# The entry of the MLP of a hybrid decoder block: a written order for ScalarE and VectorE, five operations on GpSimd, and another first product

## The chip, the cores and the metric

The kernel runs on one core of one Trainium2 chip. The metric is the device time of one execution in microseconds. A core has TensorE (matmuls, which read SBUF and write PSUM), VectorE and ScalarE (elementwise work on SBUF and PSUM), GpSimd (elementwise work on SBUF; it also issues some DMAs) and SyncE (which issues the other DMAs). Each engine works through its own queue in order and waits on semaphores of the others.

## The reference

One decoder layer on a sequence of 1024 tokens with 1024 channels, float32. Only the end of it matters here:

```python
mix = jnp.concatenate([att, conv, pool], axis=-1)
x = x + mix @ w_out[l]
h2 = rms_norm(x, norm2_g[l])
up = h2 @ w_up[l]                       # 1024 x 5632
up = causal_depthwise_conv(up, ffn_dw_w[l])   # width 3
gate, val = jnp.split(up, 2, axis=-1)
x = x + (jax.nn.silu(gate) * val) @ w_down[l]
```

## The kernel before

Products of float32 are made of three matmuls (`mm3`, lines 53 to 55): each operand is split into a rounded high half and the rest, the low half (`split`: line 48, a cast on ScalarE; line 49, a subtraction, on VectorE unless another engine is given), and high x high, high x low and low x high are added up in PSUM.

The up-projection of the MLP is made block by block: `up(f)` for 22 blocks `f` of 128 gate and 128 value channels. Each block's four quarter products (two halves of the tokens, two halves of the channels) are made from seven products instead of eight, by sums and differences of the quarters (a Strassen scheme). So the activations are needed in four raw quarters and in differences of them: `hq["11"]`, `hq["2"]`, `hq["3"]` and `hq["21"]` hold t1, t2, t3 and t4, and `T[q]` holds the split (high, low) pairs that TensorE reads: `t11`, `t21` (raw, first half of the tokens), `t22` (raw, second half), `t1`, `t2`, `t3`, `t4`. On the weights' side `wur` is a block as loaded, `wuh`/`wul` its split raw quarters, `ws` its sums and differences, `wsh`/`wsl` the split of these. One product is `prod`: four channel chunks of three matmuls, twelve matmuls of 128x512.

Ahead of the blocks stands the entry, a loop over eight token tiles `t` of 128 tokens (`c` in the profile is the output projection's last part, `x` and `x2s` its residual sum). `h2T(t)` normalises a tile and transposes it:

- line 702, the tile is stored to DRAM by GpSimd's queue; line 704, its square sum on ScalarE; lines 85 and 86, the inverse root on GpSimd (`ss`); line 706, the normalised tile `xh` on VectorE;
- line 712, eight transposes on TensorE into two PSUM banks (`d` in the profile, `pq[0]` and `pq[1]` in the code), four each;
- for tiles 0 to 3 the splits of t11 and t21 and a copy; for tiles 4 to 7 a copy to t3 (line 722, ScalarE), t1 (a subtraction, line 677), the split of t22, then t2, t3 and t4 (subtractions, line 677). In the profile all four arrays are called `h`; in the lists of order below they are `h_5422` (t1), `h_5428` (t2), `h_5429` (t3) and `h_5423` (t4).

The two transpose banks are used in turn, so a tile's transposes wait until the tile before has been read from the same bank.

At the last tile, before its `h2T`, block 0's two products that need only the first tokens are issued (t11 and t21), and the columns of the first three late tiles (0:384) of t2, t1 and t3 are split. The last 128 columns are split in `up(0)`, together with `ws` and t4. Block 0 then makes the products t2, t1, t3, t22, t4. The PSUM pool `psO` of the odd blocks takes the banks that the transposes leave.

The order on each engine is set by a scheduler which places the instructions by its own timeline and by the order in which they are written; an engine in a `manual_schedule` keeps the written order. The written order holds on SyncE alone, and there only in the down-projection. Pools have a fixed number of buffers per tag (`s8` six, `ep` four, `hx` eight, `mx` two and four), and a buffer is taken again when its last reader is done.

Of the kernel before, what the change touches and what calls it, by code (L numbers as in the profile page):

```python
# [16 lines left out]
P = 128  # L17
# [22 lines left out]
def tile_hybrid_block(ctx: ExitStack, tc: tile.TileContext, x: bass.AP, xT: bass.AP, prm: bass.AP,  # L40
# [635 lines left out]
    def sub(out, a, b):  # L676
        nc.vector.tensor_tensor(out=out, in0=a, in1=b, op=ALU.subtract)  # L677
# [17 lines left out]
    def psum(f):  # L695
        pool = psE if f % 2 == 0 else psO
        return [pool.tile([P, 512], F32, name=n, tag=n) for n in ("b1", "b2", "b3")]

    def h2T(t):
        xh = cp.tile([P, D], F32, name="xh")  # L700
        xs = x2[t // 2][:, (t % 2) * D:(t % 2) * D + D]
        nc.gpsimd.dma_start(out=x2d[t], in_=xs)
        ss = cp.tile([P, 1], F32, name="ss2")
        nc.scalar.activation(out=xh, in_=xs, func=AF.Square, accum_out=ss)
        rsqrt(ss, ss, D, 1)
        nc.vector.scalar_tensor_tensor(out=xh, in0=xs, scalar=ss, in1=g2b, op0=ALU.mult, op1=ALU.mult)
        ts = slice((t % 4) * P, (t % 4) * P + P)
        pq = []
        for q in range(2):
            ps = psD.tile([P, 512], F32, name="d", tag="d")  # L710
            for j in range(4):
                nc.tensor.transpose(out=ps[:, j * P:(j + 1) * P], in_=xh[:, (q * 4 + j) * P:(q * 4 + j + 1) * P],
                                    identity=ident)
            pq.append(ps.rearrange("p (k n) -> p k n", k=4))
        if t < 4:
            for q, quad in enumerate(("11", "21")):
                hi, lo = T[quad]
                split(hi[:, :, ts], lo[:, :, ts], pq[q])
                nc.scalar.copy(out=hq[quad][:, :, ts], in_=pq[q])
        else:  # L720
            t1, t2, t3, t4 = [hq[q][:, :, ts] for q in ("11", "2", "3", "21")]
            nc.scalar.copy(out=t3, in_=pq[0])
            sub(t1, pq[0], t1)
            hi, lo = T["22"]
            split(hi[:, :, ts], lo[:, :, ts], pq[1])
            sub(t2, pq[1], t1)
            sub(t3, pq[1], t3)
            sub(t4, t4, t2)

    SKEW = 2  # L730
    load_up(0)
# [3 lines left out]
    for t in range(NT):  # L735
        mix_att(t, 1)
        if t + SKEW < NT:
            mix_att(t + SKEW, 0)
        if t == NT - 1:
            bank0 = psum(0)  # L740
            prod(bank0[0], hl[0][0], 0, "11", True, True)
            prod(bank0[1], hl[0][0], 1, "21", True, True)
            T["2"] = (slot(s8, "s8", "t2h", F32R), slot(s8, "s8", "t2l", F32R))
            T["1"] = (slot(s8, "s8", "t1h", F32R), slot(s8, "s8", "t1l", F32R))
            T["3"] = (slot(s8, "s8", "t3h", F32R), slot(mxa, "mx", "t3l", F32R))
            for q, src in (("2", "2"), ("1", "11"), ("3", "3")):
                split(T[q][0][:, :, 0:384], T[q][1][:, :, 0:384], hq[src][:, :, 0:384])
# [5 lines left out]


    ep = mlp.enter_context(tc.tile_pool(name="ep", bufs=4, **left))
    psO = ps_ctx.enter_context(tc.tile_pool(name="psO", bufs=1, space=PSUM))

    def ex(name, dtype=F32):
        return slot(ep, "ep", name, dtype)

    def split_sums(f):
        hi, lo = ex("wsh", F32R), ex("wsl", F32R)
        split(hi, lo, ws[f])
        hl[f].append((hi, lo))

    def taps3(ac, us, e, f):
        w0 = PC_FW + (e * NF + f) * 3
# [3 lines left out]
                                           op0=ALU.mult, op1=ALU.add)  # L771

    def up(f):
        b1, b2, b3 = bank0 if f == 0 else psum(f)
        raw_hl = hl[f][0]
        u = ex("u").rearrange("p (e h) n -> p e (h n)", e=2)
        ug, uv = u[:, 0], u[:, 1]
# [4 lines left out]
        if f > 0:  # L782
            prod(b2, raw_hl, 1, "21", True, True)
        nc.vector.tensor_tensor(out=ug[:, h0], in0=ug[:, h0], in1=b2, op=ALU.add)
        if f == 0:
            split_sums(0)
            r = slice(384, 512)
            split(T["2"][0][:, :, r], T["2"][1][:, :, r], hq["2"][:, :, r])
            split(T["1"][0][:, :, r], T["1"][1][:, :, r], hq["11"][:, :, r])
            split(T["3"][0][:, :, r], T["3"][1][:, :, r], hq["3"][:, :, r])  # L790
# [247 lines left out]
```

## Time and profile before

| | |
|---|---|
| median of 3 runs | 1162.03 us (1159.37 to 1162.38) |
| profiled execution | 1161.21 us, its span 1159.4 us |
| busy in the span | TensorE 1104.9, VectorE 882.5, ScalarE 576.0, GpSimd 361.4 us |
| granted TensorE clock, mean | 0.982 |
| entry: tile 4's transposes to block 1's first product of sums | 480.9 to 526.1 us |
| TensorE busy from 526.1 to 926 | 398.7 of 399.9 us |

Times in the rows of a timeline are microseconds from the start of the span: start, length, engine, line, operation, output and inputs by the program's names, shapes, a count where several like instructions stand in one row, and in brackets how long the engine had been idle before, and for whom it waited. In rows of groups the columns are the line, engine, operation, names and shapes with a count, then busy time and the mean of one in ns, then the idle time before.

### The profile page before, as it was taken

Reading aid. Unit: us, or ns where it says so; the run is one execution under the profiler, and the core shown is the slowest. Engines: PE = TensorE matmul, PEld = TensorE weight load, DVE = VectorE, ACT = ScalarE, POOL = GpSimd, SP = SyncE. Lnnn points to the kernel's source line nnn. Section 1 sums busy time; section 2 is a strip of 40 time slices with the busy share of each in tenths; the row PEclk is TensorE's granted clock in tenths of the full one; section 3 lists DMA queues with packets and bytes.
Section 4 is the critical chain, followed back from the end, with each engine's and each line's share of the span. In section 5 each row is a group of like instructions: output and inputs, shape, how many; then the busy total and the mean of one; then the engine's idle time right before and its main releaser. Section 6 shows DMA issues by size and latency. Waiting matters only on the chain.

```text
span 1159.4 us, 15556 instructions
## 1 busy us (share of the span) xinstructions
PE 1104.9 (95%) x5684; PEld 921.4 (79%) x5684; DVE 882.5 (76%) x1259; ACT 576.0 (50%) x1045; POOL 361.4 (31%) x373
## 2 busy tenths in 40 slices
PE   7999889999999999879999999999999999899996
PEld 6789889978778878758888888888888788688875
DVE  5798974758998756778877888787878755998673
ACT  8322456688998644445443535353535343233331
POOL 1365597867666653101212121212121210000010
PEclk9999999999999999969999999999999999899999
DMA  9220110022111141211222121312221397672372
GB/s 359 72 81 25 40 28 20 15 74 74 55 48 46 47 154 73 109 37 55 89 75 96 68 96 68 105 59 85 79 98 67 117 328 267 240 263 91 128 235 74
DMA packets 51885, 119.99 MB, mean 103 GB/s; under 512 B 6368, under 2 KB 11872, under 8 KB 48992
## 3 DMA queue, kind: packets, MB, share of 16 engines
q1 hardware_dynamic: 46208, 99.06, 25.8%
q0 software_dynamic: 5600, 19.93, 4.3%
q8 instruction: 45, 0.74, 0.3%
q14 instruction: 32, 0.26, 0.1%
HBM read 94.84 MB, written 19.92 MB: 99 GB/s over the span
## 4 chain that ended last, share of the span: by engine, by line
PE 69%; DVE 10%; issue 7%; DMA 5%; ACT 4%; POOL 3%; SPq 1%; POOLq 0%; ACTq 0%; DVEq 0%
PE b L53 12%; PE b L55 12%; PE b L54 12%; PE mm L53 3%; PE mm L55 3%; PE mm L54 3%; DVE dl L49 3%; PE s L499 2%; DVE acc L257 2%; PE t L523 2%; DMA dr<-in_w_down_dram 2%; PE c L53 1%; PE c L55 1%; PE c L54 1%; DMA dr<-gd 1%
## 5 line engine op out<-in xcount | busy, mean ns | idle before, releaser
L814 POOL TENSOR_TENSOR ac<-ac 128x1024 f32<-128x1024 f32 x22 | 61.5, 2793 | 367.9 <-ACT u L795 207.3
L770 DVE SCALAR_TENSOR_TENSOR ac<-u,par,ac 128x1023 f32<-128x1023 f32 x88 | 112.7, 1280 | 9.6 <-ACT ac L768 8.7
L53 PE MATMUL mm<-w,hh 128*128 128x256 f32 (+1 forms) x384 | 110.3, 288 | 8.5 <-DVE qk L445 4.6
L54 PE MATMUL mm<-w,hh 128*128 128x256 f32 (+1 forms) x384 | 109.5, 285 | 0.6 <-POOL w L49 0.6
L55 PE MATMUL mm<-w,hl 128*128 128x256 f32 (+1 forms) x384 | 109.1, 284 | 0.0
L48 ACT CAST wsh<-ws 128x2048 fp32r<-128x2048 f32 x22 | 42.0, 1910 | 123.5 <-PE b L54 123.3
L257 DVE SCALAR_TENSOR_TENSOR acc<-u,par,acc 128x512 f32<-128x512 f32 x120 | 93.3, 835 | 0.0
L49 DVE TENSOR_TENSOR dl<-dr,dh 128x1024 fp32r<-128x1024 f32 (+1 forms) x39 | 65.6, 1684 | 28.0 <-ACT dh L48 24.9
L511 POOL TENSOR_TENSOR p<-p,l 128x896 f32<-128x896 f32 (+3 forms) x64 | 72.6, 1151 | 44.0 <-DVE l L510 37.5
L48 ACT CAST dh<-dr 128x1024 fp32r<-128x1024 f32 (+1 forms) x39 | 54.7, 1401 | 58.4 <-PE y L55 24.7
L53 PEld LDWEIGHTS mm<-w,hh 128*128 128x128 f32 x384 | 73.0, 190 | 10.1 <-DVE fgt L433 4.8
L49 POOL TENSOR_TENSOR w<-wr,w 128x256 fp32r<-128x256 f32 (+1 forms) x56 | 63.9, 1166 | 42.6 <-ACT w L48 42.3
L54 PEld LDWEIGHTS mm<-w,hh 128*128 128x128 f32 x384 | 73.1, 190 | 1.2 <-POOL w L49 0.8
L55 PEld LDWEIGHTS mm<-w,hl 128*128 128x128 f32 x384 | 73.2, 191 | 0.3
L864 POOL DMA_DIRECT2D out_dram<-acc x16 | 8.7, 542 | 206.9 <-DVE acc L860 206.3
L54 PE MATMUL x<-dl,dh 128*128 128x512 f32 x176 | 69.6, 395 | 3.4 <-DVE dl L49 3.4
L55 PE MATMUL x<-dh,dl 128*128 128x512 f32 x176 | 69.3, 394 | 0.0
L768 ACT ACTIVATE ac<-u,par 128x1024 f32<-128x1024 f32 x44 | 50.7, 1152 | 36.3 <-DVE u L805 35.8
L48 ACT CAST dh<-res 128x1024 fp32r<-128x1024 f32 x22 | 23.1, 1051 | 84.2 <-PE y L55 55.7
L49 DVE TENSOR_TENSOR wsl<-ws,wsh 128x2048 fp32r<-128x2048 f32 x22 | 50.4, 2290 | 12.4 <-ACT wsh L48 12.4
L677 DVE TENSOR_TENSOR ws<-wur 128x512 f32<-128x512 f32 x22 | 59.1, 2688 | 0.0
L53 PE MATMUL x<-dh 128*128 128x512 f32 x176 | 54.0, 402 | 5.2 <-DVE acc L860 4.5
(308 smaller groups left out, 3395.1 us busy)
## 6 DMA issues: line engine op xcount, KB each, us to landing
wur<-in_w_up_dram SPq DMA_DIRECT2D x22, 1024.0 KB, 4.9
dr<-in_w_down_dram SPq DMA_DIRECT2D x66, 256.0 KB, 5.1
dr<-gd SPq DMA_DIRECT2D x55, 256.0 KB, 4.3
gd<-ac POOLq DMA_DIRECT2D x22, 512.0 KB, 3.0
res<-gd SPq DMA_DIRECT2D x22, 256.0 KB, 5.6
wr<-in_w_in_dram SPq DMA_DIRECT2D x40, 128.0 KB, 2.1
v<-in_x_dram SPq DMA_DIRECT2D x8, 512.0 KB, 8.4
wor<-in_w_out_dram SPq DMA_DIRECT2D x16, 256.0 KB, 3.0
```

Of the source, the lines that this page charges most:

```text
L48: nc.scalar.copy(out=dst_hi, in_=src)
L49: (lo or nc.vector).tensor_tensor(out=dst_lo, in0=src, in1=dst_hi.bitcast(F32), op=ALU.subtract)
L53: nc.tensor.matmul(ps, a_hi, b_hi, start=first, stop=False, skip_group_check=more)
L54: nc.tensor.matmul(ps, a_hi, b_lo, start=False, stop=False, skip_group_check=more)
L55: nc.tensor.matmul(ps, a_lo, b_hi, start=False, stop=last, skip_group_check=more)
L257: nc.vector.scalar_tensor_tensor(out=a, in0=u[:, c, o + j:o + j + 512], scalar=pc(PC_DW + c * CW + j), in1=a, op0=ALU.mult, op1=ALU.add)
L499: nc.tensor.matmul(ps[:, 0:c1 - c0], qT[:, i * P:(i + 1) * P], part[:, c0:c1], start=b == 0, stop=b == 1 and c1 < n)
L511: nc.gpsimd.tensor_tensor(out=pt[:, 0:n], in0=pt[:, 0:n], in1=l[:, 1:2].broadcast_to([P, n]), op=ALU.mult)
L677: nc.vector.tensor_tensor(out=out, in0=a, in1=b, op=ALU.subtract)
L768: nc.scalar.activation(out=ac, in_=us, func=AF.Copy, scale=pc(w0 + 2))
L770: nc.vector.scalar_tensor_tensor(out=ac[:, j:S], in0=us[:, 0:S - j], scalar=pc(w0 + 2 - j), in1=ac[:, j:S], op0=ALU.mult, op1=ALU.add)
L814: nc.gpsimd.tensor_tensor(out=a[:, 1], in0=a[:, 1], in1=a[:, 0], op=ALU.mult)
```

## The change

From the last token tile on, ScalarE and VectorE get the written order (`manual_schedule`), which ends inside `up(0)`. `last_tile` writes it out: the split of block 0's `ws` first, its low half on GpSimd; then the old columns of t2; then the last tile's own steps with t22 and t2 ahead of t3 and t1. For tiles 4 to 7 the difference of t4 goes to GpSimd (four operations of 128x512). t1 is split behind t2, t3 whole (2048 columns) in `up(0)`, behind the load and the raw split of block 1, which `up(0)` now has ahead of its products. Block 0's product t22 comes first, into a PSUM bank of its own (`b22`, in `psO`, whose waits are now by tile), and is added to `u` by one more VectorE operation. `wsh`/`wsl` of all blocks move from pool `ep` to `s8`, t3's split pair from `s8` and `mx` to `ep`, t1's low half to `mx`.

```diff
@@ h2T
+        if t == NT - 1:
+            return pq
...
-            sub(t4, t4, t2)
+            nc.gpsimd.tensor_tensor(out=t4, in0=t4, in1=t2, op=ALU.subtract)
+
+    def split_sums(f, lo=None):
+        pair = slot(s8, "s8", "wsh", F32R), slot(s8, "s8", "wsl", F32R)
+        split(*pair, ws[f], lo)
+        hl[f].append(pair)
+
+    banks, region = [], ExitStack()
+
+    def last_tile(t):
+
+        old, new = slice(0, 384), slice(384, 512)
+        banks.extend(psum(0))
+        T["2"] = (slot(s8, "s8", "t2h", F32R), slot(s8, "s8", "t2l", F32R))
+        T["1"] = (slot(s8, "s8", "t1h", F32R), slot(mxa, "mx", "t1l", F32R))
+        (h2, l2), (h1, l1), (h22, l22) = T["2"], T["1"], T["22"]
+        t1, t2, t3, t4 = [hq[q][:, :, new] for q in ("11", "2", "3", "21")]
+        region.enter_context(tc.manual_schedule(engines={mybir.EngineType.Activation, mybir.EngineType.DVE}))
+        pq = h2T(t)
+        prod(banks[0], hl[0][0], 0, "11", True, True)
+        prod(banks[1], hl[0][0], 1, "21", True, True)
+        split_sums(0, nc.gpsimd)
+        split(h2[:, :, old], l2[:, :, old], hq["2"][:, :, old])
+        nc.scalar.copy(out=t3, in_=pq[0])
+        sub(t1, pq[0], t1)
+        nc.scalar.copy(out=h22[:, :, new], in_=pq[1])
+        sub(t2, pq[1], t1)
+        nc.scalar.copy(out=h2[:, :, new], in_=t2)
+        sub(l22[:, :, new], pq[1], h22[:, :, new].bitcast(F32))
+        sub(l2[:, :, new], t2, h2[:, :, new].bitcast(F32))
+        sub(t3, pq[1], t3)
+        nc.scalar.copy(out=h1[:, :, old], in_=hq["11"][:, :, old])
+        nc.scalar.copy(out=h1[:, :, new], in_=t1)
+        sub(l1[:, :, old], hq["11"][:, :, old], h1[:, :, old].bitcast(F32))
+        sub(l1[:, :, new], t1, h1[:, :, new].bitcast(F32))
+        nc.gpsimd.tensor_tensor(out=t4, in0=t4, in1=t2, op=ALU.subtract)
...
         if t == NT - 1:
-            bank0 = psum(0)
-            prod(bank0[0], hl[0][0], 0, "11", True, True)
...
+            last_tile(t)
+            break
...
-    psO = ps_ctx.enter_context(tc.tile_pool(name="psO", bufs=1, space=PSUM))
+    psO = ps_ctx.enter_context(tc.tile_pool(name="psO", bufs=1, space=PSUM, reuse_waits="tile"))
...
@@ up
+        sums = hl[f][1]
         if f == 0:
-            split_sums(0)
...
+            load_up(1)
+            split_raw(1)
+            T["3"] = (ex("t3h", F32R), ex("t3l", F32R))
+            split(*T["3"], hq["3"])
             T["4"] = (hx("t4h", F32R), hx("t4l", F32R))
             split(*T["4"], hq["21"])
+            add_sums(1, ex("ws"))
+            region.close()
+
+            b22 = psO.tile([P, 512], F32, name="b2", tag="b2")
+            prod(b22, sums, 3, "22", True, True)
...
-        if f + 1 < NF:
+        if 0 < f < NF - 1:
...
-        prod(b3, sums, 3, "22", False, True)
+        if f == 0:
+            nc.vector.tensor_tensor(out=ug[:, h1], in0=ug[:, h1], in1=b22, op=ALU.add)
+        else:
+            prod(b3, sums, 3, "22", False, True)
```

What this does to the queues, at three places. TensorE, behind the transposes of the last three tiles (`b_5875` to `b_5877` are block 0's banks, `b_6054` and `b_6055` block 1's, `b_5976` the new bank), as a piece of the difference:

```order
 L712 MATMUL d<-ident,xh 128x128 x24
-L53 MATMUL b_6054<-t11h,wuh 128x512
-L54 MATMUL b_6054<-t11l,wuh 128x512
-L53 MATMUL b_6055<-t21h,wuh 128x512
-L54 MATMUL b_6055<-t21l,wuh 128x512
+L53 MATMUL b_5976<-t22h,wsh 128x512
+L54 MATMUL b_5976<-t22l,wsh 128x512
+L55 MATMUL b_5976<-t22h,wsl 128x512
```

Four matmuls of block 1 stood there, followed by one of t1 and one of t2; now t22's twelve stand first, then the one of t1, then all of t2, then t1.

VectorE from tile 6 on, before:

```order
L677 TENSOR_TENSOR h_5423<-h_5423,h_5428 128x4x128
L677 TENSOR_TENSOR h_5422<-d,h_5422 128x4x128
L706 SCALAR_TENSOR_TENSOR xh<-x2s,ss_5916,g2b 128x1024
L49 TENSOR_TENSOR t22l<-d,t22h 128x4x128
L677 TENSOR_TENSOR h_5428<-d,h_5422 128x4x128
L677 TENSOR_TENSOR h_5429<-d,h_5429 128x4x128
L677 TENSOR_TENSOR h_5423<-h_5423,h_5428 128x4x128
L677 TENSOR_TENSOR h_5422<-d,h_5422 128x4x128
L49 TENSOR_TENSOR t2l<-h_5428,t2h 128x4x384
L49 TENSOR_TENSOR t22l<-d,t22h 128x4x128
L677 TENSOR_TENSOR h_5428<-d,h_5422 128x4x128
L677 TENSOR_TENSOR h_5429<-d,h_5429 128x4x128
```

and now:

```order
L706 SCALAR_TENSOR_TENSOR xh<-x2s,ss_5886,g2b 128x1024
L677 TENSOR_TENSOR h_5422<-d,h_5422 128x4x128
L49 TENSOR_TENSOR t22l<-d,t22h 128x4x128
L677 TENSOR_TENSOR h_5428<-d,h_5422 128x4x128
L677 TENSOR_TENSOR h_5429<-d,h_5429 128x4x128
L49 TENSOR_TENSOR t2l<-h_5428,t2h 128x4x384
L677 TENSOR_TENSOR h_5422<-d,h_5422 128x4x128
L677 TENSOR_TENSOR h_5428<-d,h_5422 128x4x128
L677 TENSOR_TENSOR t22l<-d,t22h 128x4x128
L677 TENSOR_TENSOR t2l<-h_5428,t2h 128x4x128
L677 TENSOR_TENSOR h_5429<-d,h_5429 128x4x128
L677 TENSOR_TENSOR t1l<-h_5422,t1h 128x4x384
```

The differences of t4 (`h_5423`) are gone, the old columns of t2 (`t2l`, 384 wide) stand ahead of the last tile's first sub, and the sum of `u` and `wsl`, which followed the last row before, stand later or on GpSimd.

GpSimd from the root of the last tile but one to the first product `ac`, now:

```order
L86 TENSOR_TENSOR ss_5839<-ss_5839,nhalf 128x1
L730 TENSOR_TENSOR h_5423<-h_5423,h_5428 128x4x128
L85 TENSOR_SCALAR ss_5886<-ss_5886 128x1
L86 TENSOR_TENSOR ss_5886<-ss_5886,nhalf 128x1
L730 TENSOR_TENSOR h_5423<-h_5423,h_5428 128x4x128
L49 TENSOR_TENSOR wsl<-ws,wsh 128x2048
L730 TENSOR_TENSOR h_5423<-h_5423,h_5428 128x4x128
L765 TENSOR_TENSOR h_5423<-h_5423,h_5428 128x4x128
L847 TENSOR_TENSOR ac<-ac 128x1024
```

Of these only the three rows of `ss` and the last one stood there before. ScalarE, for its part, has the cast `wsh` directly behind the last tile's Square (line 704), ahead of tile 6's copy to t3; before it stood behind the last tile's `t22h`.

More of the change, by code (lines that the diff above doesn't have):

```diff
@@ L739, in tile_hybrid_block @@
         if t == NT - 1:
-            bank0 = psum(0)
-            prod(bank0[0], hl[0][0], 0, "11", True, True)
[L742 to L747, printed above, removed]
+            last_tile(t)
+            break
         h2T(t)
@@ L755, in tile_hybrid_block @@
     ep = mlp.enter_context(tc.tile_pool(name="ep", bufs=4, **left))
-    psO = ps_ctx.enter_context(tc.tile_pool(name="psO", bufs=1, space=PSUM))
+    psO = ps_ctx.enter_context(tc.tile_pool(name="psO", bufs=1, space=PSUM, reuse_waits="tile"))
     def ex(name, dtype=F32):
         return slot(ep, "ep", name, dtype)
[L761 to L764, printed above, removed]
     def taps3(ac, us, e, f):
@@ L773, in up @@
     def up(f):
-        b1, b2, b3 = bank0 if f == 0 else psum(f)
+        b1, b2, b3 = banks if f == 0 else psum(f)
         raw_hl = hl[f][0]
@@ L784, in up @@
         nc.vector.tensor_tensor(out=ug[:, h0], in0=ug[:, h0], in1=b2, op=ALU.add)
+        sums = hl[f][1]
         if f == 0:
-            split_sums(0)
[L787 to L790, printed above, removed]
+            load_up(1)
+            split_raw(1)
+            T["3"] = (ex("t3h", F32R), ex("t3l", F32R))
+            split(*T["3"], hq["3"])
             T["4"] = (hx("t4h", F32R), hx("t4l", F32R))
             split(*T["4"], hq["21"])
-        sums = hl[f][1]
+            add_sums(1, ex("ws"))
+            region.close()
+            b22 = psO.tile([P, 512], F32, name="b2", tag="b2")
+            prod(b22, sums, 3, "22", True, True)
         prod(b1, sums, 1, "2", False, True)
```

## The prediction

> **What bounds the kernel now.** I read the page's slices first, then busy time by stage, then TensorE's waits in the stage of the change, then the engines' timelines there. Busy time by stage (length, then busy time and count of PE, PEld, DVE, ACT and POOL, then the granted clock, DMA share and GB/s):
>
> ```profile
> 486.00:499.20 13.20, 5.05 (x26) 3.39 (x25) 12.94 (x19) 8.92 (x12) 0.74 (x2) 0.65 0.00 0
> 499.20:510.40 11.20, 7.32 (x16) 5.26 (x17) 11.20 (x12) 5.25 (x6) 0.00 (x0) 0.50 0.00 1
> 510.40:526.10 15.70, 15.70 (x69) 12.81 (x68) 9.44 (x9) 6.93 (x7) 0.00 (x0) 1.00 0.19 68
> 526.10:926.00 399.90, 398.70 (x1730) 324.57 (x1729) 320.82 (x268) 179.12 (x187) 71.60 (x42) 1.00 0.23 83
> ```
>
> From 510.4 to 926 TensorE is busy all but 1.2 us, so any time won ahead of that reaches the end. Ahead of it, VectorE is busy 24.14 of 24.4 us and TensorE's clock is halved: the entry is VectorE's chain. TensorE waits there for these (total, times, longest), and its timeline is:
>
> ```profile
> PE b L53 <- DVE h L677: 3.9, 1, 3.9
> PE b L54 <- DVE t1l L49: 3.9, 1, 3.9
> 494.18 1.09 PE L712 MATMUL d<-ident,xh 128*128 128x128 f32 x4 [0.71 <-DVE h L677]
> 499.20 0.77 PE L53 MATMUL b<-t11h,wuh 128*128 128x512 f32 x1 [3.93 <-DVE h L677]
> 505.98 0.79 PE L54 MATMUL b<-t1l,wsh 128*128 128x512 f32 x1 [3.88 <-DVE t1l L49]
> 507.00 0.63 PE L53 MATMUL b<-t1h,wsh 128*128 128x512 f32 x1
> 507.42 0.63 PE L54 MATMUL b<-t1l,wsh 128*128 128x512 f32 x1
> 523.40 0.39 PE L53 MATMUL b<-t4h,wuh 128*128 128x512 f32 x1
> 523.63 0.39 PE L54 MATMUL b<-t4l,wuh 128*128 128x512 f32 x1
> 526.12 0.40 PE L53 MATMUL b<-t1h,wsh 128*128 128x512 f32 x1
> ```
>
> Six matmuls run from 499.20; the stream is unbroken only from 505.98, at 0.42 us each while the clock is halved (507.00 to 507.42), 0.23 later (523.40 to 523.63). My mark is 526.12, where channel block 1 starts its t1 product: 84 matmuls, seven products, stand between the last transposes and it in both kernels.
>
> VectorE, ScalarE and GpSimd in the entry, of before:
>
> ```profile
> 488.57 1.28 DVE L677 TENSOR_TENSOR h<-d,h 128x512 f32<-128x512 f32 x2
> 490.37 0.68 DVE L677 TENSOR_TENSOR h<-d,h 128x512 f32<-128x512 f32 x1
> 490.97 1.27 DVE L706 SCALAR_TENSOR_TENSOR xh<-x2s,ss,g2b 128x1024 f32<-128x1024 f32 x1
> 492.76 1.27 DVE L677 TENSOR_TENSOR h<-d,h 128x512 f32<-128x512 f32 x2
> 495.50 1.76 DVE L49 TENSOR_TENSOR t2l<-h,t2h 128x1536 fp32r<-128x1536 f32 x1 [0.26 <-ACT t2h L48]
> 497.17 0.68 DVE L49 TENSOR_TENSOR t22l<-d,t22h 128x512 fp32r<-128x512 f32 x1
> 499.57 2.28 DVE L49 TENSOR_TENSOR wsl<-ws,wsh 128x2048 fp32r<-128x2048 f32 x1
> 503.57 2.35 DVE L49 TENSOR_TENSOR t1l<-h,t1h 128x1536 fp32r<-128x1536 f32 x2
> 487.71 1.07 ACT L704 ACTIVATE xh<-x2s 128x1024 f32<-128x1024 f32 x1
> 488.81 0.59 ACT L722 COPY h<-d 128x512 f32<-128x512 f32 x1
> 493.99 1.48 ACT L48 CAST t2h<-h 128x1536 fp32r<-128x1536 f32 x1
> 495.37 0.59 ACT L48 CAST t22h<-d 128x512 fp32r<-128x512 f32 x1
> 496.32 1.92 ACT L48 CAST wsh<-ws 128x2048 fp32r<-128x2048 f32 x1
> 489.23 0.55 POOL L86 TENSOR_TENSOR ss<-ss,nhalf 128x1 f32<-128x1 f32 x1
> ```
>
> **The change, part by part.** An instruction starts some 0.1 us ahead of the recorded end of the one in front, as these rows do.
>
> *Four differences to GpSimd.* VectorE loses four ops of 0.68 us. Between the sub that ends at 489.85 and the last tile's `xh` at 490.97 stood one of them and tile 6's first sub; now `xh` follows at once, since the root ends at 489.78: 489.82 to 491.1, 1.15 earlier. GpSimd's first two differences have no reader before t4.
>
> *The cast `wsh` earlier.* ScalarE makes it (1.92) at 488.81, right behind the last Square, without a wait, where the copy `h` of tile 6 stood. That copy moves to 490.6 to 491.2, and tile 6's four VectorE ops follow it: 491.2 to 493.7, against 490.37 to 494.03 before. So the gain in front is nearly paid back: the last four transposes start 0.3 earlier, 493.85 to 494.95, `t2h` (1.48) runs 493.15 to 494.65, and `t22h` ends at 495.6.
>
> *The low half `wsl` on GpSimd.* This shape is not in the trace for GpSimd. The nearest rows (min/median/max in ns) and what happens when both engines read SBUF:
>
> ```profile
> L49 POOL TENSOR_TENSOR wo<-wor,wo x16: 1279/1298/1717, 254.5 to 439.9; 128x512 fp32r<-128x512 f32 x16
> L814 POOL TENSOR_TENSOR ac<-ac x22: 2386/2838/2845, 532.1 to 935.5; 128x1024 f32<-128x1024 f32 x22
> 532.13 2.76 POOL L814 TENSOR_TENSOR ac<-ac 128x1024 f32<-128x1024 f32 x1 [42.35 <-DVE ac L770]
> 531.95 0.69 DVE L684 TENSOR_TENSOR ws<-wur 128x512 f32<-128x512 f32 x1
> 532.56 2.89 DVE L677 TENSOR_TENSOR ws<-wur 128x512 f32<-128x512 f32 x1
> L677 DVE TENSOR_TENSOR ws<-wur 128x512 f32<-128x512 f32 x20 | 57.8, 2889 | 0.0
> L49 DVE TENSOR_TENSOR pt<-t,pt 128x512 fp32r<-128x512 f32 x48 | 32.7, 684 | 1.8 <-ACT pt L48 1.5
> ```
>
> 512 columns take 1.28 alone and 1024 take 2.39, so 2048 take 2.39 + 2 x 1.11 = 4.6 us (an estimate; the ends are 4.2, by the 2.25 that the op at 532.13 took once VectorE's op ended at 532.64, and 5.7, twice the median; I take the straight line, since both its points are the fastest of their shapes). A VectorE op with two SBUF inputs that starts beside a GpSimd one is held until that ends: 2.89 for 0.69, ending 0.56 behind GpSimd's 534.89, in all 20 cases. Ops that read PSUM keep 0.684 (`pt`, in the attention, beside GpSimd's work there). So GpSimd's second difference waits for `xh` until 491.1 and ends at 492.3; `wsl` runs 492.3 to 496.9. Tile 6's four ops read PSUM and pass. `t2l` of the old columns has two SBUF inputs: ready at 494.65, it is held to 496.9 and ends at 496.9 + 1.76 - 0.13 = 498.5 (0.13 is what 0.56 lacks of 0.69). Behind it in VectorE's queue stand two subs and `t22l`, 0.6 apart: `t22l` ends at 500.35.
>
> *Last quadrant's product first, in a bank of its own.* It needs `t22h` (495.6), `wsl` (496.9), `t22l` (500.35). TensorE issues one matmul at 495.7, stalls, and streams from 500.4. Before, its first products had to wait for the release of a transpose bank (499.20) and then for `t1l`. Next needs: `t2l` of the new columns, held by GpSimd's last difference (499.75 to 501.05), ends at 501.6; `h<-d` to 502.2 and both `t1l` (2.35) to 504.5, wanted 11 slow and fast matmuls of t22 and 13 of t2 after 500.4, at 507.7. Then the sum into `u` (0.68) and `wul` (1.76, of the row's 128x1536 shape) to 507, wanted at 510.6; t3l and t4l, 2.28 each, to 511.4, wanted at 512.6 and 518. All covered by the stream, with some 3 us of slack at `t1l`; if that cover goes, `t1l` is late next.
>
> *Further edits, taken at nothing.* t1 and t3 split later, t3 in one piece, one more VectorE sum (0.68, `b22` into `u`): VectorE idles 6.3 us of the third stage. `wsh`/`wsl` change places with t3 in the pools; each still has one buffer per block. SP's queue keeps its order, and POOL's stores `gd` stand behind `wsl` and the differences, whose last ends at 501.05 while the first product `ac` starts at 532.13.
>
> **The sum.** The unbroken stream starts at 500.4 instead of 505.98: 5.6 us. One matmul is done ahead of it instead of six: 5 x 0.23 = 1.15 back. The slow stretch I take as long as before, ten matmuls. Gain 4.4 us. The profiled execution took 1161.21 (span 1159.4), which gives 1156.8; the median of the runs lies 0.8 above it, which gives 1157.6. I say 1157.2.
>
> The clock: here it was restored some 4.4 us into the stream (0.50 up to 510.40, 1.00 after). [...]
>
> **Rivals.**
> [...]
> (2) GpSimd's third difference (1.3) gets in between `wsl` and `t2l`: all of it 1.3 later, gain 3.1: 1158.5. The row at 532.13 shows an engine getting in between two ops of the other.
> (3) No change: the stream starts early but breaks once for over 3 us, at `t1l` or in the block loop, whose order moved: the slack there is what I worked out, not what a row shows. 1161.
> (4) Slower, by one mechanism: GpSimd starved, which the trace has:
>
> ```profile
> 99.55 12.91 POOL L49 TENSOR_TENSOR w<-wr,w 128x256 fp32r<-128x256 f32 x3 [16.75 <-ACT w L48]
> 99.12 11.34 DVE L257 SCALAR_TENSOR_TENSOR acc<-u,par,acc 128x512 f32<-128x512 f32 x17
> ```
>
> Three small ops took 12.91 us while VectorE ran 17 two-input ops on end. If `wsl` gets no turn until VectorE's row of low halves breaks, at t4l, which waits for GpSimd's last difference, that is near 506.3 (from 494.65 its ops end to end, unheld): `wsl` ends at 510.9, and the product now first in TensorE's order stands still until then. The mark comes at 510.9 + 82 x 0.23 + 2 = 531.8: 1166.9. It decides from a `wsl` that ends later than 505 (no gain), and past 508.4 it is slower. Against it: at 492.3 VectorE is in ops on PSUM, which leave the turn free. [...]
>
> **How the numbers follow.** Forecast 0.55, rivals 0.15, 0.15, 0.09, 0.06. About 0.3% (3.5 us) can be told from no change: below 1158.5 is faster. The forecast's own range, with the ends of `wsl` (-0.4 to +1.1) and of the clock, is 1155.7 to 1159; some 0.85 of it is faster, so is rival 1, and 0.4 of rival 2: 0.68. Same: 0.26, slower: 0.06. The range 1154 to 1161 leaves out rival 4 and part of rival 3 and of rival 1's fast end.
>
> **What would show it.** `wsl` as one GpSimd op of 4.6 us, ending near 497; `t2l` of 1536 columns as a VectorE row near 3.9 us; TensorE's stream unbroken from about 500.4 and block 1's t1 product near 521.7; 100% TensorE after. Wrong if `t22l` ends before 499 or after 502, if TensorE has a second wait over 1 us before the mark, or if the loop shows waits that it lacked.

## The result, and the profile after

The changed kernel takes 1153.53 us (median of four runs, 1152.8 to 1155.28) against 1162.2 (1159.37 to 1162.59): ratio 0.9933, interval 0.9913 to 0.9952. On another occasion it was 1154.3 against 1161.03: 0.9928 (0.9908 to 0.9949). So 6.7 to 8.7 us are won; the forecast was 4.4, at 1157.2, in a range of 1154 to 1161. The first median lies 0.5 below that range, the second 0.3 inside its lower end.

Busy time by stage, in the columns of the prediction. The stages are those of before, cut anew: the third is as long as before and ends where block 1's t1 product starts, and the first two share what lies ahead of it:

```profile
484.80:497.98 13.18, 5.88 (x27) 3.66 (x25) 11.66 (x13) 7.40 (x10) 10.14 (x5) 0.65 0.00 0
497.98:505.00 7.02, 6.05 (x20) 4.86 (x21) 6.93 (x8) 6.67 (x7) 1.33 (x2) 0.69 0.00 0
505.00:520.70 15.70, 14.96 (x66) 11.92 (x65) 13.73 (x14) 8.40 (x9) 0.00 (x0) 1.00 0.19 68
520.70:921.00 400.30, 399.14 (x1742) 326.43 (x1741) 321.95 (x268) 179.38 (x188) 71.45 (x42) 1.00 0.23 84
```

The third stage starts at 505.0, where it started at 510.4, although TensorE now idles for 0.74 us in it; 1.24 of these 5.4 us lie ahead of the entry, as is shown below. TensorE is busy 6.05 of 7.02 us in the second stage, where it was 7.32 of 11.2, and the granted clock there is 0.69, where it was 0.50. GpSimd has 10.1 us in the first stage, where it had 0.74. TensorE's waits in the entry and its rows there:

```profile
PE b L54 <- DVE t22l L677: 2.9, 1, 2.9
PE b L53 <- DVE u L833: 0.7, 1, 0.7
493.44 1.08 PE L712 MATMUL d<-ident,xh 128*128 128x128 f32 x4 [0.77 <-DVE h L677]
495.22 0.79 PE L53 MATMUL b<-t22h,wsh 128*128 128x512 f32 x1 [0.70 <-ACT t22h L755]
498.95 0.79 PE L54 MATMUL b<-t22l,wsh 128*128 128x512 f32 x1 [2.94 <-DVE t22l L677]
502.43 0.39 PE L53 MATMUL b<-t22h,wsh 128*128 128x512 f32 x1
520.68 0.39 PE L53 MATMUL b<-t1h,wsh 128*128 128x512 f32 x1
```

One matmul, a wait for `t22l`, then a stream from 498.95 that breaks once, for 0.74. VectorE, GpSimd and ScalarE there:

```profile
488.61 2.29 DVE L706 SCALAR_TENSOR_TENSOR xh<-x2s,ss,g2b 128x1024 f32<-128x1024 f32 x1
492.02 1.27 DVE L677 TENSOR_TENSOR h<-d,h 128x512 f32<-128x512 f32 x2
494.23 2.67 DVE L49 TENSOR_TENSOR t2l<-h,t2h 128x1536 fp32r<-128x1536 f32 x1 [0.94 <-ACT t2h L48]
498.22 0.68 DVE L677 TENSOR_TENSOR t22l<-d,t22h 128x512 fp32r<-128x512 f32 x1
500.73 2.35 DVE L677 TENSOR_TENSOR t1l<-h,t1h 128x1536 fp32r<-128x1536 f32 x2
488.55 1.27 POOL L730 TENSOR_TENSOR h<-h,h 128x512 f32<-128x512 f32 x1
489.78 5.51 POOL L49 TENSOR_TENSOR wsl<-ws,wsh 128x2048 fp32r<-128x2048 f32 x1
495.25 2.78 POOL L730 TENSOR_TENSOR h<-h,h 128x512 f32<-128x512 f32 x1
494.58 0.59 ACT L755 CAST t22h<-d 128x512 fp32r<-128x512 f32 x1
```

Each engine holds the other by turns. `xh`, a 1.28 us operation, takes 2.29 because GpSimd's difference started 0.06 ahead of it and ran to 489.82 (with the differences on VectorE it takes 1.28, below); `wsl`, whose row starts at 489.78, waits for `xh` until 490.90 and then takes 4.4 of its own (it ends 4.39 behind `xh` here, and 4.39 behind it with the differences on VectorE too); `t2l` (1.76 of its own) ends 1.6 behind `wsl`'s 495.29; and GpSimd's third difference (1.28 of its own) waits for `t2l`.

To see where the 8.4 us between the two spans (1159.4 and 1151.0) came from, take three places in each trace: the entry's first transposes, block 1's first t4 product (from there both make the same products, in an order that differs by a few matmuls a block), and the first matmul of the down-projection. Before:

```profile
451.44 0.82 PE L712 MATMUL d<-ident,xh 128*128 128x128 f32 x6
542.76 0.39 PE L53 MATMUL b<-t4h,wuh 128*128 128x512 f32 x1
928.60 0.39 PE L53 MATMUL x<-dh 128*128 128x512 f32 x1
```

After:

```profile
450.20 0.82 PE L712 MATMUL d<-ident,xh 128*128 128x128 f32 x6
537.19 0.39 PE L53 MATMUL b<-t4h,wuh 128*128 128x512 f32 x1
920.99 0.39 PE L53 MATMUL x<-dh 128*128 128x512 f32 x1
```

| stretch | before | after | won |
|---|---|---|---|
| ahead of the entry | 451.44 | 450.20 | 1.24 |
| entry, to block 1's t4 product | 91.32 | 86.99 | 4.33 |
| block loop, to the down-projection | 385.84 | 383.80 | 2.04 |
| behind it, to the span's end | 230.8 | 230.0 | 0.8 |

The first and the last line are not the change's. A kernel with the code of before up to the entry (its run is told below) has its first transposes at 450.28, and all twelve further runs have them between 449.35 and 451.95; their last stretch lies between 229.4 and 235.2, and in the second traces of the old and the new entry it is 231.8 and 232.0. The entry (3.7 by these second traces) and the loop are the change's.

### The profile page after: what moved, and what is told of

Read it like the earlier page. It is cut to its first block, busy times and chain, and to the rows that moved or that the text cites. A ratio compares the mean times of both kernels' runs of the same rounds, so it can differ in the third digit from the quotient of the medians.

```text
span 1151.0 us, 15552 instructions
## 1 busy us (share of the span) xinstructions
PE 1100.4 (96%) x5684; PEld 919.7 (80%) x5684; DVE 882.8 (77%) x1254; ACT 574.8 (50%) x1044; POOL 373.7 (32%) x378
## 4 chain that ended last, share of the span: by engine, by line
PE 64%; issue 17%; DVE 8%; DMA 4%; ACT 4%; POOL 2%; SPq 1%; POOLq 0%; ACTq 0%; DVEq 0%
PE b L53 12%; PE b L54 12%; PE b L55 12%; PE mm L53 4%; PE mm L55 4%; PE mm L54 4%; DVE acc L257 2%; PE s L499 2%; PE t L523 2%; PE c L53 1%; PE c L55 1%; PE c L54 1%; DMA dr<-in_w_down_dram 1%; PE f L53 1%; PE f L55 1%
```

## Experiments

The theory after this comparison: the entry is won because TensorE's stream starts when `t22l` is there (498.95, which is 48.76 behind the first transposes; 54.54 before); the holds between VectorE and GpSimd eat most of what the work on GpSimd frees; and the loop's 2 us have a cause of their own. The rivals stand with each run. What was measured, for all runs: the start of the stream and block 1's t4 product, both from the first transposes; the loop as above; the mean distance of matmul starts in the loop (560 to 900 us); the ratio to the kernel before, with its 95% interval. Each trace is of one execution, while the ratio is of all.

| run | stream | t4 | loop | ns | ratio (interval) |
|---|---|---|---|---|---|
| before | 54.54 | 91.3 | 385.8 | 230.4 | 1 |
| changed | 48.76 | 87.0 | 383.8 | 229.1 | 0.9933 (0.9913 to 0.9952) |
| changed again | 48.72 | 87.1 | 383.8 | 229.1 | 0.9928 (0.9908 to 0.9949) |
| `wsl` on VectorE | 50.01 | 87.7 | 383.6 | 229.1 | 0.9958 (0.9941 to 0.9974) |
| differences on VectorE | 48.91 | 87.3 | 383.9 | 229.1 | 0.9943 (0.9928 to 0.9959) |
| t22 not first | 50.67 | 89.0 | 383.6 | 229.1 | 0.9959 (0.9945 to 0.9973) |
| whole-pool waits | 50.72 | 88.5 | 383.8 | 229.1 | 0.9961 (0.9946 to 0.9975) |
| no written order | 51.57 | 91.1 | 383.8 | 229.1 | 0.9978 (0.9964 to 0.9992) |
| t22's chain first | 46.78 | 85.2 | 383.6 | 229.1 | 0.9927 (0.9913 to 0.9942) |
| no differences on GpSimd | 44.85 | 92.1 | 383.6 | 229.0 | 0.9991 (0.9980 to 1.0002) |
| sums ahead | 45.24 | 84.2 | 383.6 | 229.1 | 0.9915 (0.9892 to 0.9937) |
| before, tile waits | 54.38 | 90.8 | 385.9 | 230.4 | 1.0008 (0.9995 to 1.0021) |
| before, the pools | 53.14 | 90.0 | 383.7 | 229.1 | 0.9973 (0.9956 to 0.9990) |
| before, two low halves | 56.22 | 94.1 | 386.6 | 230.9 | 1.0049 (1.0031 to 1.0066) |

In the expectations the stream's starts are 0.24 too large (49.0 for 48.76): the first transposes had been read 0.24 early.

**`wsl` back on VectorE.**

```diff
-        split_sums(0, nc.gpsimd)
+        pair = slot(s8, "s8", "wsh", F32R), slot(s8, "s8", "wsl", F32R)
+        nc.scalar.copy(out=pair[0], in_=ws[0])
+        hl[0].append(pair)
         split(h2[:, :, old], l2[:, :, old], hq["2"][:, :, old])
+        sub(pair[1], ws[0], pair[0].bitcast(F32))
```

> Block 0's low half wsl goes back to VectorE, behind t2l of the old columns; all else as in the changed kernel (1153.5 us; t2l there 2.67 us, t22l ends at 498.90, TensorE's stream from 498.95 in a span where the entry begins 1.2 us earlier than before). Theory (hold): the 2.67 us of t2l are 1.76 of its own and 0.9 of waiting for GpSimd's wsl, so t2l falls to 1.76 and wsl takes 2.28 behind it; t22l ends 2.28 - 0.9 = 1.4 later, near 500.3; time 1154.9. Rival (full price): GpSimd took 2.28 us off the chain and t2l is long for another reason; t2l keeps 2.67, t22l ends 2.3 later, time 1155.8 or more. On the 2 us that were won in the block loop: this kernel has the loop's pools of the changed kernel; if they (or the waits of psO by tile) are the reason, the mean spacing of matmuls in the loop stays at 229.1 ns (it was 230.4 before); if it is an accident of the run, it moves between runs.

VectorE's rows:

```profile
494.48 1.76 DVE L49 TENSOR_TENSOR t2l<-h,t2h 128x1536 fp32r<-128x1536 f32 x1 [0.94 <-ACT t2h L48]
496.15 2.29 DVE L677 TENSOR_TENSOR wsl<-ws,wsh 128x2048 fp32r<-128x2048 f32 x1
499.75 0.68 DVE L677 TENSOR_TENSOR t22l<-d,t22h 128x512 fp32r<-128x512 f32 x1
```

`t2l` is back at 1.76: the 0.9 was the hold. The stream starts 1.25 later (1.4 expected). Block 1's t4 product comes 0.7 and 0.6 later than in the two traces of the changed kernel: the first of these loses 0.74 to a wait for `u` that is absent here, and in the second the clock is halved for longer (5.9 us into the stream against 3.3, last section). So GpSimd's making `wsl` is worth 1.25 us at the start of the stream and some 0.7 at block 1, of the 2.28 that it takes on VectorE. The time, 1156.15, would fit the rival, but the stretch behind the loop alone is 232.5 here against 230.0: a whole time does not tell 1 us from none, and the two theories are told apart by the rows.

**The four differences back on VectorE.**

```diff
-            nc.gpsimd.tensor_tensor(out=t4, in0=t4, in1=t2, op=ALU.subtract)
+            sub(t4, t4, t2)
...
-        nc.gpsimd.tensor_tensor(out=t4, in0=t4, in1=t2, op=ALU.subtract)
+        sub(t4, t4, t2)
```

> The four differences of t4 go back to VectorE, in the written place; wsl stays on GpSimd. Theory (hold): in the changed kernel two xh of 1.28 us took 2.3 because GpSimd's difference had started first, so each difference cost VectorE about 1.0 us instead of 0.68. Undone, xh takes 1.28 again and the differences 0.68 each: the last tile's xh ends 0.3 to 0.7 earlier, wsl (4.4 us of its own) starts earlier, t2l is held for less, and t22l ends between 0.7 earlier and 0.3 later than 498.90; time 1152.8 to 1153.8. Rival (full price): three differences stand ahead of t22l, 3 x 0.6 = 1.8 us later; time 1155.3.

All `xh` of the last two tiles (count, then min/median/max in ns), in the changed kernel and then in this one:

```profile
L706 DVE SCALAR_TENSOR_TENSOR xh<-x2s,ss,g2b x2: 2287/2298/2308, 483.4 to 488.6; 128x1024 f32<-128x1024 f32 x2
```

```profile
L706 DVE SCALAR_TENSOR_TENSOR xh<-x2s,ss,g2b x2: 1278/1278/1278, 483.7 to 488.9; 128x1024 f32<-128x1024 f32 x2
492.49 2.63 DVE L677 TENSOR_TENSOR h<-h,h 128x512 f32<-128x512 f32 x1
```

The holds at `xh` are gone, one moves to tile 6's difference (2.63, behind `wsl`), and the stream starts within 0.2 of where it did. The differences on GpSimd bring next to nothing (0.2 to 0.3 at block 1): two of them held an `xh` for 1.0 each, where each would have cost 0.68.

**t22's product last again, in the third bank.**

```diff
-            b22 = psO.tile([P, 512], F32, name="b2", tag="b2")
-            prod(b22, sums, 3, "22", True, True)
...
-        if f == 0:
-            nc.vector.tensor_tensor(out=ug[:, h1], in0=ug[:, h1], in1=b22, op=ALU.add)
-        else:
-            prod(b3, sums, 3, "22", False, True)
+        prod(b3, sums, 3, "22", False, True)
```

> Block 0's products in the old order (t2, t1, t3, t22, t4), t22 into the third bank, without the extra bank and the extra VectorE sum; everything else as in the changed kernel. Theory (the stream starts when the first product's last operand is there): t2 is now first and needs t2l of the new columns, which ended at 500.2 against 498.9 of t22l, and t1l (503.1) is wanted 24 matmuls later: the stream starts 1.3 later and does not break; time 1154.8. Rival (the order is what carries the gain): with t2 first TensorE breaks again at t1l or waits for a bank, 3 us or more as before; time 1156.5 to 1158.

TensorE's row at the start of the stream:

```profile
501.63 0.80 PE L53 MATMUL b<-t1h,wsh 128*128 128x512 f32 x1 [6.38 <-ACT t1h L762]
```

Right in kind: the stream starts 1.9 later (1.3 expected) and does not break, though the time, 1156.73, lies in the rival's range. But the operand was another than expected: in the scheduler's order one matmul of t1 stands ahead of t2 and waits for `t1h`, not for `t2l`. With the scheduler's order of the rest, the new first product is worth 1.9 us.

**t22's chain first.** ScalarE's `t22h` ahead of the copy to t3, VectorE's `t22l` behind the first sub, `t2l` of the old columns behind the others:

```diff
-        split(h2[:, :, old], l2[:, :, old], hq["2"][:, :, old])
-        nc.scalar.copy(out=t3, in_=pq[0])
+        nc.scalar.copy(out=h2[:, :, old], in_=hq["2"][:, :, old])
+        nc.scalar.copy(out=h22[:, :, new], in_=pq[1])
+        nc.scalar.copy(out=t3, in_=pq[0])
         sub(t1, pq[0], t1)
-        nc.scalar.copy(out=h22[:, :, new], in_=pq[1])
-        sub(t2, pq[1], t1)
-        nc.scalar.copy(out=h2[:, :, new], in_=t2)
         sub(l22[:, :, new], pq[1], h22[:, :, new].bitcast(F32))
-        sub(l2[:, :, new], t2, h2[:, :, new].bitcast(F32))
-        sub(t3, pq[1], t3)
+        sub(t2, pq[1], t1)
+        nc.scalar.copy(out=h2[:, :, new], in_=t2)
+        sub(t3, pq[1], t3)
+        sub(l2[:, :, old], hq["2"][:, :, old], h2[:, :, old].bitcast(F32))
+        sub(l2[:, :, new], t2, h2[:, :, new].bitcast(F32))
```

> t22's chain moved to the front of the last tile's steps: the cast t22h ahead of the copy to t3 on ScalarE, t22l directly behind the first sub on VectorE, and t2l of the old columns (the operation that is held by wsl) behind the subs of t2 and t3. Nothing else changes. Theory (hold): t22l no longer stands behind the held t2l and ends near 495.5; wsl ends at 495.3; the stream starts 3.0 to 3.4 earlier than 498.95. [...] Rival (something else is late next): the stream breaks at t2l, t1l or t3l, which now end no earlier than before, and all but 0.5 us is given back: 1153.

VectorE and TensorE:

```profile
495.88 0.69 DVE L677 TENSOR_TENSOR h<-d,h 128x512 f32<-128x512 f32 x1 [2.37 <-ACT h L754]
497.23 0.79 PE L54 MATMUL b<-t22l,wsh 128*128 128x512 f32 x1 [1.01 <-DVE t22l L677]
```

The stream starts 2.0 earlier, not 3.0: the first sub waits for ScalarE's copy to t3, which had been put behind `t22h`. Block 1 comes 1.8 earlier, so nothing else was late next. The time, 1153.18, misses 1150.2 to 1151.8, the author's estimate, and can't be told from the changed kernel's medians. Its term for the clock is shown by no run: here the matmuls start 0.43 us apart up to 501.66 and 0.23 apart from 501.92, so the slow stretch lasted 4.4 us from the start of the stream, where it was 3.3 in the changed kernel's first trace.

**No differences on GpSimd.** On top of it, with the copy to t3 and the first sub ahead of `t22h` again and the cast `t2h` behind both:

```diff
-            nc.gpsimd.tensor_tensor(out=t4, in0=t4, in1=t2, op=ALU.subtract)
...
-        nc.gpsimd.tensor_tensor(out=t4, in0=t4, in1=t2, op=ALU.subtract)
...
+            sub(hq["21"], hq["21"], hq["2"])
             T["4"] = (hx("t4h", F32R), hx("t4l", F32R))
```

> Built on the run with t22's chain first (1153.2 us; there the stream started 47.0 us after the first transposes of the entry, against 49.0 in the changed kernel). Two more steps: GpSimd makes no difference of t4 any more, VectorE makes all four as one operation of 2048 columns behind t3l, where TensorE is busy; and ScalarE keeps the copy to t3 ahead of t22h, with the cast t2h of the old columns behind both. Theory (hold): both xh fall from 2.3 to 1.28, wsl ends near 44.3 and t22l near 45.3 after the first transposes, t2l takes 1.76; the stream starts 1.7 earlier than in that run and block 0's t4 product 1.2 to 2.0 earlier; time 1151 to 1152. Rival (something else is late next): the 2.28 us on VectorE make t4l or block 1's sums late, TensorE waits over 1.5 us for t4 or for u, and the time is 1153 to 1155.

TensorE's two longest waits behind block 0, and what ScalarE did:

```profile
521.36 0.50 PE L53 MATMUL b<-t1h,wsh 128*128 128x512 f32 x1 [4.00 <-ACT wsh L48]
523.69 0.79 PE L55 MATMUL b<-t1h,wsl 128*128 128x512 f32 x1 [1.59 <-DVE wsl L49]
516.69 1.28 ACT L843 ACT_TABLE_LOAD   x1 [6.14 <-DVE ac L795]
519.41 1.90 ACT L48 CAST wsh<-ws 128x2048 fp32r<-128x2048 f32 x1
```

Both sides were right in turn. The stream starts 1.9 earlier than in the run it is built on, and block 0's t4 product 1.2 earlier. Then block 1's `wsh` stands behind a Silu that waits for VectorE's taps, which the scheduler now put ahead of block 1's sums: 5.6 us of waits, more than was won, and behind them TensorE's clock is halved once more (a stretch by the columns of the stages):

```profile
525.60:529.00 3.40, 3.40 (x10) 2.62 (x9) 3.37 (x5) 0.59 (x1) 0.58 (x1) 0.50 0.00 0
```

The rival had named block 1's sums; the time, 1158.86, is worse than its range.

**Whole-pool waits, and tile waits in the kernel before.**

```diff
-    psO = ps_ctx.enter_context(tc.tile_pool(name="psO", bufs=1, space=PSUM, reuse_waits="tile"))
+    psO = ps_ctx.enter_context(tc.tile_pool(name="psO", bufs=1, space=PSUM))
```

> The changed kernel with one word taken out: the PSUM pool psO waits as a whole pool again, not by tile. It asks where the 2 us in the block loop come from (mean spacing of matmuls 230.4 ns before, 229.1 in the changed kernel and in all four runs so far, which is 84 x 1.35 ns = 0.11 us for each of 21 blocks = 2.4 us). Theory (placing): the new homes of wsh, wsl and t3 in SBUF do it; spacing stays 229.1, the loop's length from block 1's to the last product stays 383.5. Rival (waits): the finer waits do it; spacing goes to 230.4 and the loop to 385.6, time 1155.6.

and the reverse in the kernel before:

> The kernel before with one word added: psO waits by tile. Theory (placing): spacing stays 230.4 ns, loop 385.6 us, time as before within 0.5 us (about 1161.2). Rival (waits): 229.1 ns, loop 383.5, time 1159. It is also a second trace of the unchanged entry: if the 1.2 us by which the changed kernel's trace was ahead at the first transposes (449.95 against 451.20) is an accident of that one trace of before, its first transposes come between 449.7 and 450.7, as in the four runs so far.

TensorE at the start of the stream, without the word:

```profile
500.88 0.77 PE L53 MATMUL b<-t22h,wsh 128*128 128x512 f32 x1 [6.42 <-ACT t1h L762]
```

Neither run touches the loop (229.1 and 230.4 ns, as without). In the entry, the changed kernel loses 1.5 us without the word: t22's first matmul waits 6.42 and the stream starts 2.0 later. The new bank comes from the banks that the transposes leave, and VectorE reads these last until 500.74; the profile names ScalarE's `t1h`, which ends at 500.78, and doesn't tell which of the two ends the wait. Either way the new first product needs the finer waits. The second run is also the second trace of the old entry: 90.8, with first transposes at 450.28.

**No written order.**

```diff
-        region.enter_context(tc.manual_schedule(engines={mybir.EngineType.Activation, mybir.EngineType.DVE}))
```

> The changed kernel without the written order: the scheduler orders ScalarE and VectorE in the entry; the operations on GpSimd, the pools and t22's product first stay. In its order the last xh stands behind tile 6's four operations and wul, and t1l of the old columns ahead of t22l. Theory (the order carries the entry's gain): the last transposes and t22l come later by the operations put ahead, 0.6 x 4 + 1.7 + 1.8 less the idle time between, so the stream starts 3 to 4.5 later than 49.0 after the first transposes; time 1156.5 to 1158. Rival (GpSimd's five operations and the new first product carry it): the stream starts within 1 us of the changed kernel's and the time is 1153.5 to 1154.5.

The last `xh` and the last transposes:

```profile
494.54 2.28 DVE L706 SCALAR_TENSOR_TENSOR xh<-x2s,ss,g2b 128x1024 f32<-128x1024 f32 x1 [0.44 <-POOL ss L86]
496.97 1.94 PE L712 MATMUL d<-ident,xh 128*128 128x128 f32 x8 [7.34 <-DVE xh L706]
```

Counted from the first transposes (449.89 here), the last `xh` starts 6.2 later than in the changed kernel, behind tile 6's operations and `wul`, and the stream 2.8 later (3 to 4.5 expected). Block 1 comes at 91.1, no earlier than in the kernel before (91.3 and 90.8): without the written order the entry's gain is gone, and the operations on GpSimd and the new first product bring nothing. The reverse, the written order without these, was not run, so what it is worth alone is not shown; taking away t22's first place costs 1.9 of the 4, the finer waits 1.5.

**Block 1's sums ahead.** On top of the run with t22's chain first:

```diff
+        nc.scalar.copy(out=t3, in_=pq[0])
+        sub(t1, pq[0], t1)
         nc.scalar.copy(out=h22[:, :, new], in_=pq[1])
...
-            nc.gpsimd.tensor_tensor(out=t4, in0=t4, in1=t2, op=ALU.subtract)
+            (nc.vector if t < 6 else nc.gpsimd).tensor_tensor(out=t4, in0=t4, in1=t2, op=ALU.subtract)
...
+            add_sums(1, ex("ws"))
             T["4"] = (hx("t4h", F32R), hx("t4l", F32R))
             split(*T["4"], hq["21"])
-            add_sums(1, ex("ws"))
```

> Built on the run with t22's chain first (there the stream started 47.0 us after the entry's first transposes, block 0's t4 product came at 65.3 and block 1's at 85.2; in the changed kernel 49.0, 67.6, 87.0; in the run without GpSimd's differences 64.1 and, after a wait of 4.0 for block 1's wsh, 92.1). Steps: the differences of tiles 4 and 5 on VectorE, tile 6's and the last one's on GpSimd as in the changed kernel; ScalarE's copy to t3 ahead of t22h; block 1's sums ws written ahead of the split of t4, so that block 1's wsh isn't late. Theory (hold): both xh take 1.28, the stream starts 45.3 to 46 after the first transposes, t4 of block 0 at 64.1 to 64.7, and nothing breaks for over 1 us: t4 of block 1 at 84.0 to 84.7, 2.3 to 3.0 earlier than in the changed kernel; time 2.5 us under the changed kernel's of the same job. Rival (something is late next again): block 1's wsh or wsl stops TensorE for over 1.5 us, time within 1 us of the changed kernel's.

TensorE's start of the stream and its one wait behind:

```profile
497.19 0.79 PE L54 MATMUL b<-t22l,wsh 128*128 128x512 f32 x1
519.94 0.50 PE L55 MATMUL b<-t1h,wsl 128*128 128x512 f32 x1 [1.57 <-DVE wsl L49]
```

The stream starts 3.5 earlier than in the changed kernel and block 1's t4 product 2.8 to 2.9 earlier, both as expected, though block 0's came 1.0 sooner than that and 1.57 was lost at block 1's `wsl`, as the rival had it. The medians of one occasion are 1152.91 and 1154.3, 1.4 apart where 2.5 were expected. By the trace the entry beats both kernels; by the whole time it beats the kernel before, and against the changed one the intervals overlap.

**The pools alone, in the kernel before.**

```diff
-            T["1"] = (slot(s8, "s8", "t1h", F32R), slot(s8, "s8", "t1l", F32R))
-            T["3"] = (slot(s8, "s8", "t3h", F32R), slot(mxa, "mx", "t3l", F32R))
+            T["1"] = (slot(s8, "s8", "t1h", F32R), slot(mxa, "mx", "t1l", F32R))
...
-        hi, lo = ex("wsh", F32R), ex("wsl", F32R)
+        hi, lo = slot(s8, "s8", "wsh", F32R), slot(s8, "s8", "wsl", F32R)
...
+            T["3"] = (ex("t3h", F32R), ex("t3l", F32R))
+            split(*T["3"], hq["3"])
```

> The kernel before with the changed kernel's pools alone: wsh and wsl of all blocks in s8, t1's low half in mx, t3's split pair in ep (so it is split whole, in up(0)); no written order, nothing on GpSimd, products in the old order. It asks for the block loop's 2 us. Theory (placing): mean spacing of matmuls in the loop 229.1 ns instead of 230.4, and 383.5 us instead of 385.6 from block 1's t4 product to the last product; with the entry as before, time 1159 to 1159.5 where before has 1161. Rival (the loop's order or the entry's): spacing stays 230.4, loop 385.6, time as before.

Block 1's t4 product and the first matmul of the down-projection:

```profile
540.98 0.39 PE L53 MATMUL b<-t4h,wuh 128*128 128x512 f32 x1
924.64 0.39 PE L53 MATMUL x<-dh 128*128 128x512 f32 x1
```

383.66 us of loop where before has 385.84, with TensorE as busy as before: the matmuls themselves follow each other 1.35 ns sooner. The order of the loop's operations is no rival: on VectorE, ScalarE and GpSimd, and by products on TensorE, it is the same in this trace as in that of before. So the places are the loop's gain, whole, without the rest of the change; the time agrees (1158.6, a little under what was expected, against 1161.03: by the interval 1.2 to 5.1 us less, about 1 of it from the entry).

**The changed kernel again.** No edit.

> [...]

The author's estimate was the stream at 49.0, block 1's t4 product at 87.0 and a time of 1153 to 1155. Stream 48.72, t4 product 87.1: the entry repeats to 0.1 us. The median is in that span, at 1154.3, and the gain of this occasion is 6.7, so part of the first one's 8.7 was luck.

**Two low halves change places, in the kernel before.**

```diff
-            T["1"] = (slot(s8, "s8", "t1h", F32R), slot(s8, "s8", "t1l", F32R))
-            T["3"] = (slot(s8, "s8", "t3h", F32R), slot(mxa, "mx", "t3l", F32R))
+            T["1"] = (slot(s8, "s8", "t1h", F32R), slot(mxa, "mx", "t1l", F32R))
+            T["3"] = (slot(s8, "s8", "t3h", F32R), slot(s8, "s8", "t3l", F32R))
```

> The kernel before with two buffers changing places: t1's low half goes to mx and t3's to s8 (wsh, wsl and t3's high half stay where they were). The run with all of the changed kernel's pools gave 229.08 ns between matmuls in the loop (t1 228.7, t11 227.9, t22 229.1 against 230.3, 231.2, 232.9 before) and 383.4 us of loop against 385.6. Theory (home of wsh and wsl): the pair that every block writes and reads anew does it, so here the spacing stays 230.4 ns and the loop 385.6. Rival (home of t1's and t3's low halves, read by 24 of 84 matmuls a block): spacing falls to 229.1, loop 383.5; in between, both take part. The whole time moves by no more than 2 us either way.

TensorE's start of the stream:

```profile
505.57 0.79 PE L54 MATMUL b<-t1l,wsh 128*128 128x512 f32 x1 [4.79 <-DVE t1l L49]
```

Both expectations fell. The spacing goes up, to 230.88 ns: t1's matmuls from 230.3 to 232.9, t2's from 229.0 to 232.1, t11's down from 231.2 to 229.8. The order of the loop's operations differs here from before's, but it is that of the run with t22's chain first, which has 229.1. So the homes of t1 and t3 take part, and even products whose buffers did not move (t2, t11) change their pace. t22, which reads `wsh` and `wsl`, keeps 232.8 here against 232.9 before, where the new pools gave 229.1, so the home of that pair seems to take part too. More than the two low halves may have moved: t3's high half is now the fourth of these buffers that the code takes from `s8`, not the fifth. Which property of a place counts stays open. The whole time was missed too: the scheduler took the new places as a reason to put t3's low half ahead of t1's second one, t1's second one ends at 505.51, the stream starts 1.7 later than before, and the time is 5 us longer, where 2 was said to be the most.

## Why the prediction was right, and where it was not

Direction and mechanism were right, and the size of the entry: the forecast had the stream start 48.96 behind the first transposes (500.4 less 451.44), and it starts at 48.76; it had block 1's t1 product at 521.7, which is 70.3 behind them, and it comes at 70.5 (520.68 less 450.20), 4.2 earlier than before's 74.7, where 4.4 was forecast. That it is so close is in part luck. The last transposes were later and `wsl` was earlier than written; the clock came back 3.3 us into the stream instead of 4.4, and TensorE then lost 0.74 waiting for `u`. By the second traces the entry's gain is 3.7. The forecast's own range, 1155.7 to 1159, takes in ends for the clock that no run shows; what the traces show is a clock that came back 4.4 us into the stream before, and 3.3 and 5.9 us in the two of the changed kernel. The time as a whole beat the forecast by a gain that the prediction didn't have.

- **The step that failed** is "Further edits, taken at nothing": "`wsh`/`wsl` change places with t3 in the pools; each still has one buffer per block". The places were taken to matter only for waits. They are worth 2.04 us of loop in the first two traces, and 2.2 by themselves (385.84 less 383.66). With them the sum is 6.4 instead of 4.4 and the forecast 1155.2, against medians of 1153.5 and 1154.3; what is left is of the size by which the stretches ahead of and behind the work vary.
- **Four differences to GpSimd.** Wrong in a part: "GpSimd's second difference waits for `xh`". It was the other way round; GpSimd issued its difference right behind the root that `xh` waits for. `xh` did start 1.1 earlier in the entry, as written, but it was held and ended 1.0 later than written (490.90, where the forecast's 491.1 is 489.9 in this trace, whose entry begins 1.24 earlier). The last transposes started 0.8 later than written. So the 1.15 that `xh` was to win came to nothing, and putting the differences back costs 0.3 at most. The error did not reach `wsl`: in either order `xh` and the difference stand one behind the other ahead of it, and it had its turn from 490.90, where the forecast's 492.3 is 491.1.
- **`wsl` on GpSimd.** 4.4 of its own against an estimate of 4.6. It ended 0.4 earlier than written, and `t2l` was held until then, with 2.67 for its row where 3.9 was written, because it was ready 0.8 later. Since `wsl` ended after `t2l` was ready, that slip did not reach `t22l`, which ends at 498.90 where the forecast's 500.35 is 499.1. (498.90 is below the 499 that the prediction calls a sign of being wrong, but that 499 was read in the trace of before, and is 497.8 here.)
- **Stream and slack.** TensorE had no second wait over 1 us before the mark, and the loop has no wait that it lacked (1.2 us ahead of the last block's t4 product, in both kernels); the 0.74 for `u` is small, and `t1l` was 3 us early. The slow stretch was some eight matmuls against ten.
- **Rivals.** (1), that `t2l` is not held (chance 0.15), fell: `t2l` and `xh` were held in each trace in which a GpSimd operation stood ahead of them (2.67 us for 1.76, and 2.29 for 1.28, in the changed kernel). (2) fell: the third difference waited for `t2l`, not the reverse (2.78). (3) did not come in the changed kernel, but it is what the run without differences on GpSimd met, at block 1's `wsh`. (4) fell: `wsl` ended 4.39 us behind the end of `xh`, with no sign of being starved.

## What to carry to other kernels

Work that was moved to GpSimd beside VectorE operations with two SBUF inputs was not free here: five operations, 5 us of VectorE's time, brought at most 0.3 and some 0.7 us, while taking away the written order of two engines cost 4. Look for the operand on which the first long stream of matmuls waits, put its chain first, and then look what the next block needs: a part of the chain won too early only moves the wait there. And read the loop's own rate in two traces, in ns per matmul, before giving a whole gain to the place that was edited.

## What was not expected of the hardware

The pace of matmuls in this loop, which TensorE fills, depends on where the buffers lie. With the same work, it was 229.04 to 229.12 ns in eleven traces with the new homes, whatever stood on VectorE and GpSimd, 230.41 and 230.43 in two with the old ones, and 230.88 with the low halves of t1 and t3 in each other's pools; t4's product kept 226.6 to 226.7 in every trace. Over some 1,674 matmuls the 1.35 ns are 2.3 us (2.04 and 2.18 by the loops' lengths), about half of what the entry brought. No wait shows but the 1.2 us ahead of the last block's t4 product, which both kernels have.

How long the slow clock lasts varies between traces of the same kernel. In the changed kernel's first trace, and then in its second (stretch, length, TensorE's busy time and count; the granted clock is the third number from the end):

```profile
498.95:502.10 3.15, 3.15 (x7) 2.48 (x8) 3.11 (x3) 3.15 (x5) 0.71 (x1) 0.50 0.00 0
502.20:505.60 3.40, 3.40 (x16) 2.80 (x15) 3.40 (x5) 3.40 (x3) 0.00 (x0) 0.99 0.00 0
```

```profile
498.55:501.90 3.35, 3.35 (x8) 2.67 (x9) 3.32 (x3) 3.35 (x4) 0.70 (x1) 0.50 0.00 0
501.90:504.20 2.30, 2.30 (x6) 1.77 (x6) 2.30 (x4) 2.30 (x3) 0.00 (x0) 0.50 0.00 0
504.40:507.80 3.40, 3.40 (x16) 2.79 (x15) 3.40 (x3) 2.10 (x2) 0.00 (x0) 0.99 0.00 0
```

The clock comes back at 502.3 in the one and at 504.5 in the other, 3.3 and 5.9 us after the start of the stream. What sets the difference was not shown. Block 1's t4 product came within 0.1 us in both all the same, since the trace in which the clock came back early then waited 0.74 for `u`.
